# Where the halves of the split weights lie in SBUF, in which order the short products take them, and three load buffers for four

## The chip, the cores and the metric

The kernel runs on one core of a Trainium2 chip. The time is the device time of one execution in microseconds (us); lower is better. Before the change the median of two runs is 2517.6 us (2517.24 and 2517.97).

## The reference

The reference is a two-layer decoder trunk on 256 tokens of width 2048, all in float32. The first layer mixes tokens with a Mamba-2 block, the second with causal attention over one key/value block; each is followed by a residual layer norm and a gated feed-forward block with a depthwise convolution. Cut to the matrix products, which are nearly all of the work:

```python
zxbcdt = x @ w_in                          # 2048 -> 10304   (Mamba-2)
mix    = y @ w_out                         # 4096 -> 2048
u      = causal_dwconv(x @ w_up) ; ffn = (silu(gate) * val) @ w_down   # 2048 -> 11264, 5632 -> 2048, twice
kv     = h @ w_kv ; q = h @ w_q ; mix = out @ w_o
h      = layer_norm(alpha * h + f(h))      # after each of the four blocks
```

## The kernel before, in words

**Products in three passes.** TensorE multiplies in a rounded float32 type, so every operand is split in two: a high part (the value rounded) and a low part (what the rounding left). A product is then high times high, plus low weights times high activations, plus high weights times low activations.

**Steps.** All weights are packed by the host into 881 tiles of 128 partitions by 1024 columns (512 KB each) in the order of use; one tile is one *step*. For every step `load` (L172 to L180) issues one DMA on the SP queue into a `raw` buffer. `split` (L182 to L211) makes the two parts: ScalarE copies `raw` to the rounded type into a `hi` tile (L209), VectorE subtracts it from `raw` into a `lo` tile (L210), and then the next `load` is issued. There are `RAW` = 4 `raw` buffers and `LA`+1 = 4 `hi` and 4 `lo` tiles. A load has to wait until the subtraction that last read its buffer is done; loads stand on the SP queue in program order with the few other transfers of that queue (the input `x`, the constants `cols`, the norm's vectors and residuals).

**Two kinds of chunk.** A chunk is 512 output columns; its steps run one behind the other. In mode X (`half`, L221) activations are the stationary operand and weights stream. In mode W, 560 of the 881 steps (the Mamba-2 input but for one step, keys, queries, and all but the first feed-forward chunk of each layer), weights are the stationary operand: `some` (L250) issues for one step eight products of one part. With the high part (L266) a product streams 512 columns, the high and the low activations at once; these are the *long* products. With the low part (L269) it streams only the 256 columns of the high activations; these are the *short* products. Each product is a weight load of 128x128 and a matmul.

**Order of long and short.** `kinds` (L157) and `whole` (L283) arrange that the two parts alternate in opposite order from step to step, so that equal kinds meet: in the Mamba-2 chunks sixteen short products in a row, then sixteen long ones; in the other (`paired`) W chunks thirty-two and thirty-two. In the first chunk (`calm`) they alternate eight by eight. By the program's order there are 199 runs of short products: 92 of 32, 85 of 16 and 22 of 8 (the first chunk, and where other work of TensorE stands in between).

**Addresses.** Call the place of a tile's first byte within 256 bytes of its partition its *position*, in units of 64 bytes (0 to 3); 64 float32 columns are 256 bytes (`LINE`), and each product's 128 stationary columns are 512, so products of one contiguous tile all have one position. By the allocation, the activations `hT` (first byte 21632) and the `hi` tiles (75904, then every 4096) are at position 2. The `lo` tiles begin at 92480 (then every 4352), position 1; in mode W the low part is shifted by `LINE // 2`, 128 bytes, in every second step, and so lies at positions 1, 3, 1, 3 from step to step, in the first chunk always at 3. In mode X it is shifted to position 2.

**Norms.** Behind three of the four blocks the layer norm (`Norm`, L422, put in order by `chain`, L918) turns the result into the next block's `hT`; there the steps' high and low parts are written into free parts of `hT` (`spare`), and the queues carry the residuals besides the weights.

Of the kernel before, what the change touches and what calls it, by code (L numbers as in the profile page):

```python
# [18 lines left out]
F32 = mybir.dt.float32  # L19
F32R = mybir.dt.float32r  # L20
# [4 lines left out]
P = 128  # L25
D = 2048
S = 256
# [12 lines left out]
NC = 512  # L40
HC = NC // 2
NEG = -1.0e30
LINE = 64
# [6 lines left out]
    N_COL += _n // P  # L50

LA = 3
RAW = 4
WARM0 = 18
HEAD, TAIL = 3, 4
LAST = 8
# [3 lines left out]
def chunks():  # L60

    z, b, c, dt = 0, 2 * DI, 2 * DI + NG * DS, 2 * DI + 2 * NG * DS

    def some(mode, name, layer, c0, n, nk):
        return [(mode, name, layer, c0 + i * NC, nk, False) for i in range(n)]

    def ffn(layer):
        up = [some(m, "ffn_w_up", layer, c + j * NC, 1, KD)[0] for j in range(DFF // NC)
              for m, c in (("W" if j else "X", 0), ("W", DFF))]
        return up + some("X", "ffn_w_down", layer, 0, 4, KF)  # L70

    out = some("W", "mamba_w_in", 0, b, 2, KD)
    out[0] = out[0][:5] + (True,)
    out += some("H", "mamba_w_in", 0, dt, 1, KD) + some("W", "mamba_w_in", 0, c, 2, KD)
    for g in range(NG):
        out += some("W", "mamba_w_in", 0, DI + g * NC, 1, KD) + some("W", "mamba_w_in", 0, z + g * NC, 1, KD)
    out += some("X", "mamba_w_out", 0, 0, 4, DI // P) + ffn(0)
    out += some("X", "w_kv", None, D, 1, KD) + some("W", "w_kv", None, 0, 4, KD) + some("W", "attn_w_q", 0, 0, 4, KD)
    return out + some("X", "w_kv", None, D + NC, 3, KD) + some("X", "attn_w_o", 0, 0, 4, KD) + ffn(1)
# [12 lines left out]
def yoco_kernel(ctx: ExitStack, tc: tile.TileContext, x, lmg, lmb, lfg, lfb, x_t, columns, w, out):  # L92
    nc = tc.nc
    base = ctx.enter_context(tc.tile_pool(name="base", bufs=1))
    wts = ctx.enter_context(tc.tile_pool(name="wts", bufs=LA + 1))
# [30 lines left out]
    steps, plan = [], chunks()  # L126
# [39 lines left out]
    raw_t, hi_t, lo_t = {}, {}, {}  # L166
    spare = {}
    gap = []
    calm = []
    pos = {"split": 0, "load": 0}  # L170

    def load():  # L172
        i = pos["load"]
        if i >= n_steps:
            return
        pos["load"] += 1
        t = wts.tile([P, 2, NC], F32, tag="raw", name="raw", bufs=RAW)
        for e in (slice(0, 1), slice(1, 2)) if i == 0 else (slice(0, 2),):
            nc.sync.dma_start(t[:, e], w[i][:, e])
        raw_t[i] = t  # L180

    def split():  # L182
        i = pos["split"]
        pos["split"] += 1
        t = raw_t.pop(i)
        if i in spare:
            h, l = (bufs["h"][:, k:k + 2].rearrange("p k a t -> p k (a t)") for k in (spare[i], spare[i] + 2))
        else:
            h = wts.tile([P, 2, NC], F32R, tag="hi", name="hi")
            if not gap:  # L190
                gap.append(wts.tile([P, LINE * 3 // 4], F32R, tag="gap", name="gap", bufs=1))
            l = wts.tile([P, 2 * NC + LINE], F32R, tag="lo", name="lo")
            ch, s = steps[i]
            if len(gap) < 2:
                gap.append(wts.tile([P, LINE // 4], F32R, tag="gap2", name="gap2", bufs=1))

            o = LINE // 4 if ch.mode != "W" else LINE // 2 if s % 2 or ch in calm else 0
            l = l[:, o:o + 2 * NC].rearrange("p (a n) -> p a n", a=2)
        hi_t[i], lo_t[i] = h, l
        if steps[i][0].mode == "H":  # L200
            for a, w in enumerate((h, l)):
                v = t[:, a].rearrange("p (k n) -> p k n", k=8)
                w = w.rearrange("p a (k e n) -> p (a k) e n", e=2, n=NC // 8)
                nc.scalar.copy(w[:, :, 0], v)
                nc.vector.tensor_sub(w[:, :, 1], v, w[:, :, 0].bitcast(F32))
            return load()
        for e in ((0,), (1,)) if i < 2 else ((0, 1),):
            sl = slice(e[0], e[-1] + 1)
            nc.scalar.copy(h[:, sl], t[:, sl])  # L209
            nc.vector.tensor_sub(l[:, sl], t[:, sl], h[:, sl].bitcast(F32))  # L210
        load()  # L211

    def splits(i, most=2):

        for _ in range(1 if steps[i][0] in calm else most):
            j = pos["split"]
            ahead = LA + 1 + sum(i <= k < j for k in spare)
            if j < min(i + ahead, n_steps) and (j in spare or sum(k not in spare for k in hi_t) < LA + 1):
                split()
# [30 lines left out]
    def some(ch, s, p):  # L250

        i = ch.first + s
        nj = ch.nj
        w = ((hi_t, lo_t)[p][i]).rearrange("p a (k n) -> p a k n", n=nj * P)
        k0, half = ch.place(s)
        banks = [p[:, j, :] for p in ch.part[half:] for j in range(2)]
        first = ch.kinds(s)[0] == p
        for kk in range(ch.per):
            k = k0 + kk
            a, b = divmod(kk, ch.per // 2)  # L260
            begins, ends = first and k == 0, not first and k == ch.nk - 1
            for j in range(nj):
                yield
                js = slice(j * P, (j + 1) * P)
                if p == 0:
                    nc.tensor.matmul(banks[j], w[:, a, b, js], ch.x.both(k), start=begins, stop=ends,  # L266
                                     skip_group_check=True)
                else:
                    nc.tensor.matmul(banks[j][:, :S], w[:, a, b, js], ch.x.hi(k), start=begins, stop=ends,  # L269
                                     skip_group_check=True)  # L270

    def beside(i):

# [9 lines left out]
    def whole(i):  # L283

        ch, s = steps[i]
        if ch.mode == "H":
            return beside(i)
        a, b = ch.kinds(s)
        if not ch.paired:
            order = [(s, a), (s, b)]  # L290
        elif s % 2 == 0:
            order = [(s, a), (s + 1, a)]
        else:
            order = [(s - 1, b), (s, b)]
        late = ch.paired and s % 2
        n = len(order) * ch.per * ch.nj
        c = 0
        for t, p in order:
            for _ in some(ch, t, p):
                if c == (n // 2 if late else n * 3 // 8):  # L300
                    if late:
                        done(i - 1)
                    run(mid, i)
                    splits(i)
                c += 1
        if not ch.paired or late:
            done(i)
# [274 lines left out]
    calm.append(chB[0])  # L582
    put_x(0)
    split()
    put_x(2)
    split()
    for p in range(2, 8):
        amid(p - 2, put_x, 2 * p)
# [382 lines left out]
    def gb_ffn(c):  # L971
        return pool[f"ffn{int(0 if 'ffn0' in pool else 1)}"][1].tile([P, 2, NC], F32, tag="gb", name="gb", bufs=3)

    def gb_last(c):
        return gb_ffn(c) if c < 3 else wts.tile([P, 2, NC], F32, tag="raw", name="gb", bufs=RAW)

# [152 lines left out]
    for h in range(HEADS):  # L1129
        i, j = divmod(h, 4)  # L1130
# [87 lines left out]
```

## Time and profile before

| | |
|---|---|
| median of two runs | 2517.6 us |
| the profiled execution: its own time | 2516.88 us |
| its span, first to last instruction | 2514.6 us |
| matmuls of TensorE | 13983 |
| of these long products of W steps (L266) | 4480 |
| short products of W steps (L269) | 4480 |
| splits on ScalarE (L209) and VectorE (L210) | 869 of 881 steps in the largest group |
| weight loads by DMA | 880 of 512 KB, median 3.9 us from issue to landing |

PE is TensorE's matmuls, PEld its weight loads, ACT ScalarE, DVE VectorE, POOL GpSimd, SP the queue that issues the DMAs. In the rows of a group stand line, engine, operation, tiles, the shapes, the count, and then busy us and mean ns of one. The duration of a matmul in the trace holds its way through the array; the next one begins earlier, so the pace is the distance of the starts, not the duration. In the chain of waits a row is start, length, engine and line, and the number of instructions: there the starts follow one another, and length by count is the pace. In a timeline row the length runs from the first start to the last end, one duration more than the pace alone gives. The change is far below what the page's tenths show, so those two views in short windows carry the reading.

### The profile page before, as it was taken

How to read it: one execution, taken by the hardware profiler on the slowest of the kernel's cores; microseconds unless marked ns; L12 is line 12 of the kernel's file. 1: busy time of each engine (PE TensorE's matmuls, PEld its weight loads, DVE VectorE, ACT ScalarE, POOL GpSimd, SP SyncE). 2: the span in 40 equal slices, each digit the busy share in tenths (PEclk: the TensorE clock that was granted, in tenths of full speed). 3: DMA queues.
4: the chain of work that ended last, by engine and by line, in shares of the span. 5: the costliest groups of instructions: out<-in, count | busy, mean ns of one | idle time of the engine just before them, and what ended most of it. 6: DMA issues, size and time to landing. Idle time of an engine off the chain costs nothing.

```text
span 2514.6 us, 36085 instructions
## 1 busy us (share of the span) xinstructions
PE 2502.2 (100%) x13983; PEld 2175.0 (86%) x13983; DVE 1657.7 (66%) x2140; ACT 1365.5 (54%) x1790; POOL 76.4 (3%) x96
## 2 busy tenths in 40 slices
PE   9999999999999999999999999999999999999998
PEld 8888888888888888888888888888888888888887
DVE  7878888755666767675445646645767676765545
ACT  6677787643465555554333445543556555554333
POOL 0000000000200000000000200000200000000001
PEclk9999999999999999999999999999999999999999
DMA  7656655666666555556676655556656665566664
GB/s 259 207 188 203 211 190 189 202 209 222 212 207 193 193 192 191 195 185 201 209 227 205 212 194 172 160 178 227 220 192 197 194 192 194 186 198 204 198 228 161
DMA packets 141739, 502.59 MB, mean 200 GB/s; under 512 B 15856, under 2 KB 16368, under 8 KB 141568
## 3 DMA queue, kind: packets, MB, share of 16 engines
q1 hardware_dynamic: 136448, 482.92, 58.8%
q0 software_dynamic: 4832, 16.85, 2.2%
q8 instruction: 109, 1.79, 0.3%
q14 instruction: 62, 0.51, 0.1%
q10 hardware_dynamic: 288, 0.52, 0.1%
HBM read 491.77 MB, written 8.45 MB: 199 GB/s over the span
## 4 chain that ended last, share of the span: by engine, by line
PE 99%; DMA 0%; DVE 0%; SPq 0%; issue 0%; ACT 0%
PE acc L266 40%; PE acc L269 20%; PE acc L231 11%; PE acc L232 11%; PE acc L236 11%; PE acc L804 1%; PE tp L406 0%; PE tp L236 0%; PE tp L232 0%; PE tp L231 0%; DMA raw<-in_w 0%; PE tp L813 0%; PE acc L787 0%; PE tp L1083 0%; PE tp L1117 0%; PE tp L1109 0%
## 5 line engine op out<-in xcount | busy, mean ns | idle before, releaser
L210 DVE TENSOR_TENSOR lo<-raw,hi 128x1024 fp32r<-128x1024 f32 (+1 forms) x869 | 1059.6, 1225 | 726.5 <-ACT hi L209 598.5
L209 ACT CAST hi<-raw 128x1024 fp32r<-128x1024 f32 (+1 forms) x869 | 909.1, 1049 | 832.0 <-PE acc L236 366.8
L266 PE MATMUL acc<-hT,hi 128*128 128x512 f32 x4480 | 1058.3, 391 | 0.9 <-ACT hi L209 0.4
L266 PEld LDWEIGHTS acc<-hT,hi 128*128 128x128 f32 x4480 | 826.3, 188 | 165.6 <-ACT hi L209 1.8
L269 PEld LDWEIGHTS acc<-hT,lo 128*128 128x128 f32 x4480 | 543.4, 188 | 15.5 <-issue 1.2
L269 PE MATMUL acc<-hT,lo 128*128 128x256 f32 x4480 | 549.5, 278 | 0.0
L232 PE MATMUL acc<-lo,gT 128*128 128x512 f32 (+1 forms) x678 | 254.5, 378 | 0.0
L231 PE MATMUL acc<-hi,gT 128*128 128x512 f32 (+1 forms) x678 | 254.1, 377 | 0.0
L236 PE MATMUL acc<-hi,gT 128*128 128x512 f32 (+1 forms) x678 | 200.8, 377 | 0.0
L232 PEld LDWEIGHTS acc<-lo,gT 128*128 128x128 f32 x678 | 127.6, 188 | 23.2
L231 PEld LDWEIGHTS acc<-hi,gT 128*128 128x128 f32 x678 | 127.6, 188 | 23.1
L236 PEld LDWEIGHTS acc<-hi,gT 128*128 128x128 f32 x678 | 124.9, 188 | 23.9
L232 PE MATMUL acc<-lo,yT 128*128 128x512 f32 (+1 forms) x270 | 98.6, 369 | 0.0
L231 PE MATMUL acc<-hi,yT 128*128 128x512 f32 (+1 forms) x270 | 98.5, 369 | 0.0
L231 PE MATMUL acc<-hi,hT 128*128 128x512 f32 x192 | 78.8, 410 | 0.0
L236 PE MATMUL acc<-hi,yT 128*128 128x512 f32 (+1 forms) x270 | 77.7, 369 | 0.0
L232 PE MATMUL acc<-lo,hT 128*128 128x512 f32 x192 | 75.4, 393 | 0.0
L636 DVE SCALAR_TENSOR_TENSOR g<-u,cols,g 128x254 f32<-128x254 f32 (+1 forms) x176 | 73.3, 477 | 2.8 <-ACT g L631 2.7
L609 DVE TENSOR_TENSOR u<-u,acc 128x512 f32<-128x512 f32 x108 | 73.4, 681 | 2.3 <-ACT u L608 1.4
L1033 ACT CAST gT<-v 128x512 fp32r<-128x512 f32 x44 | 27.3, 621 | 84.5 <-DVE v L1032 84.5
L636 DVE SCALAR_TENSOR_TENSOR v<-u,cols,v 128x254 f32<-128x254 f32 (+1 forms) x176 | 73.1, 478 | 0.0
L468 POOL TENSOR_TENSOR rs<-rs,mhalf 128x1 f32<-128x1 f32 x8 | 7.4, 930 | 1984.9 <-DVE nb L469 1984.9
(223 smaller groups left out, 1910.7 us busy)
## 6 DMA issues: line engine op xcount, KB each, us to landing
raw<-in_w SPq DMA_DIRECT2D x880, 512.0 KB, 3.9
mA<-acum_d POOLq DMA_DIRECT2D x16, 512.0 KB, 6.4
hres<-r POOLq DMA_DIRECT2D x12, 512.0 KB, 6.8
r<-hres SPq DMA_DIRECT2D x12, 512.0 KB, 4.6
eA<-acum_d POOLq DMA_DIRECT2D x16, 128.0 KB, 7.3
r<-in_x SPq DMA_DIRECT2D x4, 512.0 KB, 5.5
gb<-in_ln_mix_g SPq DMA_DIRECT2D x8, 256.0 KB, 5.2
gb<-in_ln_mix_b SPq DMA_DIRECT2D x8, 256.0 KB, 5.4
```

The costliest lines, as they stand in the source:

```text
L209: nc.scalar.copy(h[:, sl], t[:, sl])
L210: nc.vector.tensor_sub(l[:, sl], t[:, sl], h[:, sl].bitcast(F32))
L231: nc.tensor.matmul(a, th, h[:, kk, sl], start=k == 0, stop=False)
L232: nc.tensor.matmul(a, th, l[:, kk, sl], start=False, stop=False)
L236: nc.tensor.matmul(a, ch.x.lo(k)[:, ts], h[:, kk, sl], start=False, stop=k == ch.nk - 1)
L266: nc.tensor.matmul(banks[j], w[:, a, b, js], ch.x.both(k), start=begins, stop=ends, skip_group_check=True)
L269: nc.tensor.matmul(banks[j][:, :S], w[:, a, b, js], ch.x.hi(k), start=begins, stop=ends, skip_group_check=True)
L468: nc.gpsimd.tensor_tensor(self.rs[:, h, :], self.rs[:, h, :], mhalf[:, 0, :], op=OP.pow)
L609: nc.vector.tensor_add(dst, dst, p[:, :, :S])
L636: nc.vector.scalar_tensor_tensor(d, u[:, i % 2, :S - k], c1(self.at_w, w[n - 1 - k] + self.ia + i), d, op0=OP.mult, op1=OP.add)
L804: nc.tensor.matmul(ps[64 * q:64 * q + 64, c, j * P:(j + 1) * P], G[g]["xdt"][:, c, h * 64:(h + 1) * 64], G[g]["A", c][:, h, :], start=True ...
L1033: nc.scalar.copy(h, v[:, sl])
```

## The change

Three things change in the code.

1. `RAW` goes from 4 to 3: one `raw` buffer of 4096 bytes a partition less. The four `hi` tiles grow by 1024 bytes each, so `lo` and everything behind it stays where it was; the `hi` tiles lie 5120 bytes apart and still begin at position 2.
2. In mode W the `lo` tile is two halves of 544 columns, of which 512 are used: the first half of every step lies at position 1 and the second at position 3. `some` takes the eight short products in the order 0, 1, 4, 5, 2, 3, 6, 7, so their positions are 1, 1, 3, 3, 1, 1, 3, 3 in every step, the first chunk's too.
3. In the W steps whose high part is used right behind short products (every second step of the Mamba-2 chunks, every fourth of the paired ones: 180 steps) the high part is laid out in four pieces of 256 columns. The first piece begins `o`, the second `e`, the third and fourth `d` further, each with a position of its own out of four: 64 combinations, drawn by a hash of the step's number. Two products fall to each piece; their order is as before. ScalarE's copy and VectorE's subtraction take the tile in four pieces of 256 there; numbers of instructions, sizes and waits stay.

```diff
-RAW = 4
+RAW = 3
...
-            h = wts.tile([P, 2, NC], F32R, tag="hi", name="hi")
+            h = wts.tile([P, 2 * NC + 4 * LINE], F32R, tag="hi", name="hi")
+            ch, s = steps[i]
+            if ch.mode == "W" and s % (4 if ch.paired else 2) == (2 if ch.paired else 1):
+                o, d, e = (LINE // 4 * ((i * 2654435761 >> 9) // 4 ** m % 4) for m in range(3))
+                e += HC
+                d += NC
+                while d < 2 * e:
+                    d += LINE
+                while o + 2 * d > 2 * NC + 4 * LINE:
+                    d -= LINE // 4
+                h = h[:, o:o + 2 * d].rearrange("p (a n) -> p a n", a=2)[:, :, :2 * e]
+                h = h.rearrange("p a (b n) -> p a b n", b=2)[:, :, :, :HC]
+            else:
+                h = h[:, :2 * NC].rearrange("p (a n) -> p a n", a=2)
...
-            o = LINE // 4 if ch.mode != "W" else LINE // 2 if s % 2 or ch in calm else 0
-            l = l[:, o:o + 2 * NC].rearrange("p (a n) -> p a n", a=2)
+            if steps[i][0].mode == "W":
+                l = l.rearrange("p (a n) -> p a n", a=2)[:, :, :NC]
+            else:
+                l = l[:, LINE // 4:LINE // 4 + 2 * NC].rearrange("p (a n) -> p a n", a=2)
...
+            u, v, r = t[:, sl], h[:, sl], l[:, sl]
+            if len(h.shape) == 4:
+                u, r = (y.rearrange("p a (b n) -> p a b n", b=2) for y in (u, r))
+            nc.scalar.copy(v, u)
+            nc.vector.tensor_sub(r, u, v.bitcast(F32))
...
+        order = [(a, b, j) for a in range(2) for b in range(ch.per // 2) for j in range(nj)]
+        if p == 1:
+            order = [order[i] for i in (0, 1, 4, 5, 2, 3, 6, 7)]
+        for a, b, j in order:
+            yield
+            k = k0 + a * (ch.per // 2) + b
```

More of the change, by code (lines that the diff above doesn't have):

```diff
@@ L192, in split @@
             l = wts.tile([P, 2 * NC + LINE], F32R, tag="lo", name="lo")
-            ch, s = steps[i]
             if len(gap) < 2:
                 gap.append(wts.tile([P, LINE // 4], F32R, tag="gap2", name="gap2", bufs=1))
-            o = LINE // 4 if ch.mode != "W" else LINE // 2 if s % 2 or ch in calm else 0
-            l = l[:, o:o + 2 * NC].rearrange("p (a n) -> p a n", a=2)
+            if steps[i][0].mode == "W":
+                l = l.rearrange("p (a n) -> p a n", a=2)[:, :, :NC]
+            else:
+                l = l[:, LINE // 4:LINE // 4 + 2 * NC].rearrange("p (a n) -> p a n", a=2)
         hi_t[i], lo_t[i] = h, l
@@ L208, in split @@
             sl = slice(e[0], e[-1] + 1)
-            nc.scalar.copy(h[:, sl], t[:, sl])
-            nc.vector.tensor_sub(l[:, sl], t[:, sl], h[:, sl].bitcast(F32))
+            u, v, r = t[:, sl], h[:, sl], l[:, sl]
[3 more added lines that the diff above has]
+            nc.vector.tensor_sub(r, u, v.bitcast(F32))
         load()
@@ L253, in some @@
         nj = ch.nj
-        w = ((hi_t, lo_t)[p][i]).rearrange("p a (k n) -> p a k n", n=nj * P)
+        w = (hi_t, lo_t)[p][i]
+        if len(w.shape) == 3:
+            w = w.rearrange("p a (b n) -> p a b n", b=2)
         k0, half = ch.place(s)
@@ L257, in some @@
         first = ch.kinds(s)[0] == p
-        for kk in range(ch.per):
-            k = k0 + kk
-            a, b = divmod(kk, ch.per // 2)
-            begins, ends = first and k == 0, not first and k == ch.nk - 1
[L262 to L270, printed above, removed]
+        order = [(a, b, j) for a in range(2) for b in range(ch.per // 2) for j in range(nj)]
[4 more added lines that the diff above has]
+            k = k0 + a * (ch.per // 2) + b
+            begins, ends = first and k == 0, not first and k == ch.nk - 1
+            c, j0 = divmod(b * nj * P + j * P, HC)
+            js = slice(j0, j0 + P)
+            if p == 0:
+                nc.tensor.matmul(banks[j], w[:, a, c, js], ch.x.both(k), start=begins, stop=ends,
+                                 skip_group_check=True)
+            else:
+                nc.tensor.matmul(banks[j][:, :S], w[:, a, c, js], ch.x.hi(k), start=begins, stop=ends,
+                                 skip_group_check=True)
     def beside(i):
```

## The prediction

> **What bounds the kernel now.** I read the page first, for the bound and the clock, then the waits of TensorE.
>
> ```profile
> span 2514.6 us, 36085 instructions
> PE 2502.2 (100%) x13983; PEld 2175.0 (86%) x13983; DVE 1657.7 (66%) x2140; ACT 1365.5 (54%) x1790; POOL 76.4 (3%) x96
> PEclk9999999999999999999999999999999999999999
> PE 99%; DMA 0%; DVE 0%; SPq 0%; issue 0%; ACT 0%
> L266 PE MATMUL acc<-hT,hi 128*128 128x512 f32 x4480 | 1058.3, 391 | 0.9 <-ACT hi L209 0.4
> L269 PE MATMUL acc<-hT,lo 128*128 128x256 f32 x4480 | 549.5, 278 | 0.0
> ...
> PE tp L581 <- POOL ident masks.py:199: 1.4, 1, 1.4
> PE acc L266 <- ACT hi L209: 0.4, 1, 0.4
> PE acc L266 <- DVE hT L569: 0.3, 1, 0.3
> ```
>
> TensorE is the chain from end to end, at full clock. The last three rows are all that it waited for in the whole execution: 2.1 us, all at the start. So no transfer and no other engine can give time back; the change can win only in the pace of the products themselves, and it can lose wherever it makes TensorE wait. A busy 100% does not say that this pace is the best one. For that I read the chain of waits in a paired W stage and in a Mamba-2 stage, and the timeline inside two runs.
>
> ```profile
> 806.71 3.66 PE acc L269 x32
> 810.38 7.28 PE acc L266 x32
> ...
> 337.19 1.85 PE acc L269 x16
> 339.04 3.65 PE acc L266 x16
> ...
> 20.15 0.94 PE acc L269 x8
> ```
>
> ```profile
> 806.55 0.99 PE L269 MATMUL acc<-hT,lo 128*128 128x256 f32 x7
> 808.06 1.18 PE L269 MATMUL acc<-hT,lo 128*128 128x256 f32 x9
> 810.21 1.32 PE L266 MATMUL acc<-hT,hi 128*128 128x512 f32 x5
> 812.28 1.75 PE L266 MATMUL acc<-hT,hi 128*128 128x512 f32 x7
> ```
>
> A timeline row holds one duration besides its paces (278 and 391 ns by the two groups). The run's first seven short products come every (990 - 278) / 6 = 119 ns; nine from the later part every (1180 - 278) / 8 = 113 ns. The long run's first five come every (1320 - 391) / 4 = 232 ns, seven later ones every (1750 - 391) / 6 = 226.5 ns. So there are two paces for one shape, a slow one where a run begins and a fast one. As floors I take 226.6 ns and half of it, 113.3. Then the 32 short products lose 3.66 - 32 x 0.1133 = 0.034 us, the 16 lose 1.85 - 16 x 0.1133 = 0.037, so a run loses about 36 ns whatever its length, and eight of one position lose 0.94 - 0.906 = 0.034. The 32 long ones lose 7.28 - 7.25 = 0.03 us, the 16 lose 3.65 - 3.626 = 0.024: 28 ns a run. That is what the change can reach: 199 x 36 ns = 7.2 us in the short runs and 180 x 28 ns = 5.0 us in the long runs whose first step is cut in pieces, 0.5% of the time together.
>
> **The change part by part. Short products.** Nothing is added or removed: 4480 products with the same operands; weight loads read other addresses in another order. Today a run's first eight lie at one position and the slow pace lasts through these eight, to be gone at the ninth, where the position moves by 128 bytes; it does not come back at the 17th or 25th, where it moves again. After the change it moves at the third. If the move ends the slow pace, two products at 119 and one or two on the way down are left, some 10 of the 36 ns, and 199 x 26 ns = 5.2 us are saved. The other bound is that the slow pace ends by itself after eight; or, worse, that moving every two products keeps it up. For this the trace has a row of a kind: in the last steps of a mode X block products of 256 columns whose operands are all at position 2 run at a slow pace that never ends:
>
> ```profile
> 663.24 0.28 PE L231 MATMUL acc<-hi,yT 128*128 128x256 f32 x1
> 663.36 0.28 PE L232 MATMUL acc<-lo,yT 128*128 128x256 f32 x1
> 663.48 0.28 PE L231 MATMUL acc<-hi,yT 128*128 128x256 f32 x1
> 663.60 0.28 PE L232 MATMUL acc<-lo,yT 128*128 128x256 f32 x1
> ```
>
> They stand 0.12 us apart, one behind the other. All 4480 at 119 ns would be 4480 x 5.7 = 25.5 us of loss against 7.2 today, 18 us more. Bounds: -7.2 to +18 us. I take -5.2, by the nearest rows, the two inside the same run: the fast pace begins at a move of 128 bytes and outlasts two more of them.
>
> A rule of the Trainium skill speaks against all of this: "TensorE: Matmul & The Clock Gate", section "Step-by-step: what each phase is for", says that loading weights and streaming the moving operand read through two independent ports, so that the next weights' load takes nothing from the running matmul. By it no position would matter and this term would be 0. The 119 and 113 ns for one shape at one clock do not go with it, unless the slow pace is only a beginning that ends by itself.
>
> **Long products in pieces.** Again the same products; the 180 steps have up to four positions instead of one. Today's 28 ns arise at constant position 2, and they end by themselves after five products. Every place where a row shows the slow pace set in is a change between long and short, which is also a move of 64 bytes (position 2 to 1 or 3, 3 to 2); moves of 128 bytes did no harm. Of the 64 combinations half move by 64 or 192 bytes between the first two pieces, and about half end at an odd distance from position 2, where the next, uncut, step begins. Bounds: all of the 28 saved, 180 x -28 ns = -5.0 us; or all eight at 232 instead of 226.5 and another 28 ns at the next step, 8 x 5.7 + 28 - 28 = +46 ns, +8.2 us. I take +10 ns a step, +1.8 us: nearer to today's loss than to either end, and on its bad side, since the draw mixes good and bad moves and today's constant position heals after five.
>
> The cut copies cost nothing on the path: the numbers of instructions and columns are the same, ScalarE is busy 54% and VectorE 66%, and TensorE waited 0.4 us for a split in the whole run. Without that cover, a copy that took a tenth longer would be 0.1 us on 180 steps, 18 us.
>
> **One load buffer less.** A load now waits for the subtraction three steps before it, not four. Queued behind it on SP are the next loads, at the start also the last part of `x` and `cols`, and behind the blocks the norm's residuals and vectors; behind a late load wait ScalarE's copy and all that stands after it on ScalarE, then VectorE's subtraction, then TensorE.
>
> ```profile
> L179 SPq DMA_DIRECT2D raw<-in_w x882: 327/328/677, 1.3 to 2484.6; - x177
> DMA to landing us min/median/max: 3.0/3.9/9.3
> L210 DVE TENSOR_TENSOR lo<-raw,hi 128x1024 fp32r<-128x1024 f32 (+1 forms) x869 | 1059.6, 1225 | 726.5 <-ACT hi L209 598.5
> L209 ACT CAST hi<-raw 128x1024 fp32r<-128x1024 f32 (+1 forms) x869 | 909.1, 1049 | 832.0 <-PE acc L236 366.8
> ACT hi L209 <- DMA raw<-in_w: 42.0, 28, 4.3
> ```
>
> In the steady state one buffer's round is 3.9 + 1.05 + 1.23 = 6.2 us, so three buffers bring a step every 2.1 us; TensorE needs one every 2514.6 / 881 = 2.85 us. The four `hi` buffers put a split up to three steps, some 8 us, ahead of its use, so a load that lands a step later is late for ScalarE but not for TensorE. Two places have less. At the start the fourth load leaves at 4.92 today:
>
> ```profile
> 4.92 0.68 SPq L179 DMA_DIRECT2D raw<-in_w  x1
> 5.64 0.66 SPq L564 DMA_DIRECT2D x<-in_x_t  x1
> 7.51 11.75 SPq L179 DMA_DIRECT2D raw<-in_w  x5
> 3.62 7.74 DMA raw<-in_w
> ```
>
> It will leave where the fifth leaves now, at 7.51, 2.6 us later, and the last of `x` behind it. But the load of 3.62 lands only 7.74 us later, at 11.36: the transfers stand in line, and one that joins at 7.51 is still in that line. So I expect 0 to 1 us here. The other places are the three norms:
>
> ```profile
> 687.20 1.05 ACT L209 CAST hi<-raw 128x1024 fp32r<-128x1024 f32 x1 [2.01 <-DMA raw<-in_w]
> 692.12 2.11 ACT L209 CAST hi<-raw 128x1024 fp32r<-128x1024 f32 x2 [3.88 <-DMA raw<-in_w]
> ```
>
> ScalarE waits 2.0 and 3.9 us for late weights there already, and TensorE does not feel it. Bounds: nothing at both places (not below nothing: a load never leaves earlier than before), or a full shift reaching TensorE. That is two loads at the start, 2 x 2.6 us, and at each norm 3 us, less than the longest wait there: 5.2 + 9 = 14 us. I take +1 us, near the lower end, because of the steady surplus of 2.85 over 2.1.
>
> **Sum** against the profiled execution, 2516.9 us (span 2514.6 and 2.3 around it): 2516.9 - 5.2 + 1.8 + 1.0 = 2514.5. The median before is 0.7 us above that execution, so I forecast 2515.2, 2515 us.
>
> **The rivals.** (a) *The slow pace ends by itself*, after about 36 ns of loss, wherever the positions are. For it: the long runs heal at constant position, and runs of 16, of 32 and of eight lose the same 0.034 to 0.037. Against it: the eight at one position keep an average of 0.94 / 8 = 117.5 ns, so they are slow to their end, and the X rows never heal. Then the short term is 0: 2517.6 + 1.8 + 1.0 = 2520.4, slower than before. The page's rule of independent ports would come to this time too. (b) *The load ring reaches TensorE*, at the first steps and behind the three norms, with the full 14 us: 2517.6 - 5.2 + 1.8 + 14 = 2528. It decides as soon as a load that leaves later takes as long as it does now, instead of waiting less in line. The waits of 2.0 and 3.9 us behind the norm speak for it; that TensorE does not wait there at all today speaks against. (c) *The pieces keep the slow pace up* in all eight products and hand it on: 2517.6 - 5.2 + 8.2 + 1 = 2521.6. (d) *The pieces heal the long runs too*, as moves of 128 bytes do in the short ones: 2517.6 - 5.2 - 5.0 + 1 = 2508.4. That the change doesn't do what it says is excluded for the order and the addresses, which the built program fixes.
>
> **How the numbers follow.** The forecast has 0.50, and its own range is 2512 to 2518; (a) 0.17, (b) 0.10, (c) 0.10, (d) 0.13. The range reaches from (d), 2508, past (c) to 2525, which leaves out most of (b) and the case where moving every two products keeps the short ones slow, up to 2536, which I put inside (a)'s chance as its tail. A difference of 2% is 50 us, about what a measurement of this kernel can tell from no change. No term sums to that: both upper bounds of the pace and the ring together are 18 + 8 + 14 = 40 us. So within 2% has 0.97; slower 0.02, for a ring that delays TensorE in every stage; faster 0.01.
>
> **What would show it.** Right: runs of 32 short products at 3.63 to 3.64 in the chain of waits and of 16 at 1.82; wrong, if they stay at 3.66 and 1.85, or grow. The long runs behind them: 7.28 should become 7.27 to 7.31, unequal from run to run because of the draw; a constant value would say that position is nothing to them. The list of TensorE's waits should stay as short as it is; rows "PE acc L266 <- ACT hi" with more than 1 us, at 5 to 30 us or behind the norms, would show the ring. The waits of ScalarE for raw should grow from 42.0 us without harm. If TensorE's products are slower in mode X, where nothing moved, the prediction is wrong at its root.

## The result, and the profile after

The changed kernel takes 2537.84 us (two runs, 2536.64 and 2539.04) against 2517.6 us: a ratio of 1.0082, with a 95% interval of 1.0065 to 1.0098. It is 20 us slower, above the range of the prediction. The profiled execution took 2539.04 us, its span is 2536.9 us, 22.3 us more than before.

The page of the changed kernel: busy time, clock, the chain by engine, and the two groups of W products (L287 is the long one, L290 the short one).

```profile
span 2536.9 us, 36083 instructions
PE 2509.5 (99%) x13983; PEld 2174.2 (86%) x13983; DVE 1657.9 (65%) x2140; ACT 1367.6 (54%) x1790; POOL 76.1 (3%) x96
PE 87%; DMA 4%; DVE 4%; ACT 3%; issue 2%; POOL 0%; SPq 0%; ACTq 0%; DVEq 0%; POOLq 0%
L287 PE MATMUL acc<-hT,hi 128*128 128x512 f32 x4480 | 1064.4, 392 | 0.9 <-DVE hT L590 0.9
L290 PE MATMUL acc<-hT,lo 128*128 128x256 f32 x4480 | 544.6, 277 | 0.0
```

The two groups show that both kinds of product moved, in opposite ways: busy time 549.5 to 544.6 us for the short ones, 1058.3 to 1064.4 for the long ones. That nearly cancels. The new thing is the chain: TensorE holds 87% of it and not 99%; transfers, VectorE and ScalarE have come in. The waits say where: first TensorE's five longest rows (sum, count, longest, in us), then the row of ScalarE that grew most.

```profile
PE tp L427 <- POOL r L517: 4.7, 3, 1.6
PE tp L869 <- DVE sq L863: 3.6, 5, 0.9
PE tp L427 <- DVE r L501: 2.6, 2, 2.3
PE tp L427 <- issue: 1.9, 1, 1.9
PE acc L249 <- DVE hT L227: 1.5, 2, 0.8
```

```profile
ACT hi L226 <- DMA raw<-in_w: 194.6, 154, 5.2
```

Only the last of TensorE's five rows is a wait for a weight's half. L427 are the norms' transposes, L869 is the mean-square product of a Mamba-2 group, and both wait for other work of VectorE and GpSimd. The prediction had looked for the ring in rows `PE acc <- ACT hi` of more than 1 us, and there is none. ScalarE's wait for weights went from 42.0 us in 28 waits to 194.6 us in 154.

Taken product by product (both kernels issue the same 13983 matmuls in the same order; distance from one start to the next, after less before; more than 40 ns counted as a wait), the 22.3 us of the span come out so:

```
pace of the short products   -4.7 us
pace of the long products    +4.9 us
waits: start (to 13 us)      +1.0
       Mamba-2 groups        +5.6
       three norms           +2.3 +5.4 +4.9
       last chunk            +3.1
```

Of the second and the third norm's waits about 1.5 us each are not standing still: there products run at half clock behind a pause (last section).

### The profile page after: what moved, and what is told of

Read it like the earlier page. It is cut to its first block, busy times and chain, and to the rows that moved or that the text cites. A ratio compares the mean times of both kernels' runs of the same rounds, so it can differ in the third digit from the quotient of the medians.

```text
span 2536.9 us, 36083 instructions
## 1 busy us (share of the span) xinstructions
PE 2509.5 (99%) x13983; PEld 2174.2 (86%) x13983; DVE 1657.9 (65%) x2140; ACT 1367.6 (54%) x1790; POOL 76.1 (3%) x96
## 4 chain that ended last, share of the span: by engine, by line
PE 87%; DMA 4%; DVE 4%; ACT 3%; issue 2%; POOL 0%; SPq 0%; ACTq 0%; DVEq 0%; POOLq 0%
PE acc L287 35%; PE acc L290 18%; PE acc L249 10%; PE acc L248 10%; PE acc L253 10%; DMA raw<-in_w 4%; DVE lo L227 1%; ACT hi L226 1%; ACT mA L773 0%; DVE xc L657 0%; PE tp L253 0%; PE tp L249 0%; PE tp L248 0%; DMA gb<-in_ln_mix_g 0%; DVE mA L792 0%
## 5 line engine op out<-in xcount | busy, mean ns | idle before, releaser
L287 PE MATMUL acc<-hT,hi 128*128 128x512 f32 x4480 | 1064.4, 392 | 0.9 <-DVE hT L590 0.9
L287 PEld LDWEIGHTS acc<-hT,hi 128*128 128x128 f32 x4480 | 827.5, 188 | 170.0 <-ACT hi L226 1.3
L290 PEld LDWEIGHTS acc<-hT,lo 128*128 128x128 f32 x4480 | 538.8, 188 | 15.8 <-issue 0.9
L290 PE MATMUL acc<-hT,lo 128*128 128x256 f32 x4480 | 544.6, 277 | 0.0
```

Source lines behind the costliest of these rows:

```text
L287: nc.tensor.matmul(banks[j], w[:, a, c, js], ch.x.both(k), start=begins, stop=ends, skip_group_check=True)
L290: nc.tensor.matmul(banks[j][:, :S], w[:, a, c, js], ch.x.hi(k), start=begins, stop=ends, skip_group_check=True)
```

## The experiments

**One load buffer less, alone.** From the kernel before:

```diff
-RAW = 4
+RAW = 3
```

> Only one load buffer less. If the ring alone makes TensorE wait, the 22.3 us of stalls of the changed kernel come back without its other parts: 2537 to 2542 us, with TensorE waiting in front of the mean-square products of the Mamba-2 groups, in the three norms and in the last chunk. If the cut copies of the high parts delay the splits and so are needed for the stalls: 2525 or less.

Measured: 2538.11 us (four runs, 2535.83 to 2539.12), ratio 1.0081 (1.0066 to 1.0096). TensorE's longest waits:

```profile
PE tp L406 <- POOL r L496: 5.2, 3, 2.5
PE tp L848 <- DVE sq L842: 5.0, 7, 0.9
PE tp L406 <- issue: 2.3, 1, 2.3
```

The missing buffer alone makes the whole loss, at the same places: 8.9 us in the Mamba-2 groups, 9.3 in the norms, 1.9 in the last chunk by the same count. The pieces are not needed for it.

**Three buffers and the pieces, short products as before.** From the changed kernel:

```diff
-                l = l.rearrange("p (a n) -> p a n", a=2)[:, :, :NC]
+                o = LINE // 2 if s % 2 or ch in calm else 0
+                l = l[:, o:o + 2 * NC].rearrange("p (a n) -> p a n", a=2)
...
-        if p == 1:
-            order = [order[i] for i in (0, 1, 4, 5, 2, 3, 6, 7)]
```

> Three load buffers and the high parts in pieces; the short products as before. If the three parts add, the long products lose 4.9 us more than before as in the changed kernel, beside the stalls of three buffers alone (20 us, 2538.1): 2543 us, 5 us above both that run and the changed kernel. If the pieces also make the stalls longer, by slower copies: above 2547.

Measured: 2539.08 us (2538.05 to 2542.07), ratio 1.0087 (1.0072 to 1.0102). The median is 1 us above that of three buffers alone, not 5; but the runs of each spread over 3 to 4 us, so the time alone does not tell. The products do: the long ones lose 5.0 us more than before, as in the changed kernel, and the waits sum to 20.1 us as with three buffers alone (20.6). So the pieces cost pace, and no longer waits show. That execution is the longest of its four, though. If the pieces cost the 5.0 us in all of them, the waits of the median are nearer to 16 us: they differ by some us from execution to execution.

**Three buffers, the mean-square products a step later.** From the kernel with three buffers alone, all of `z_rms` to `z_split` moved by a step except in the last group:

```diff
-        at(s0 + 23, z_rms, g)
+        at(s0 + 23 + (g < NG - 1), z_rms, g)
...
```

> Three load buffers and nothing else of the change, but the mean-square products of the Mamba-2 groups (and what hangs on them) are put one step later, except in the last group. If TensorE there waits for ScalarE's and VectorE's other work that stands behind late weights, and not for the weights, one step more hides it: the stalls of 0.4 to 1.2 us in front of these products go, some 6 of the 20 us, 2532 us; the norms' and the start's stay. If the weights themselves are late, the wait moves to the next product that needs them: 2538.

Measured: 2536.75 us (four runs, 2533.73 to 2542.38), ratio 1.0083 (1.0067 to 1.01). The runs spread over 9 us, so the time does not decide between the two cases. The waits do:

```profile
PE acc L269 <- DVE lo L210: 4.0, 6, 1.2
PE tp L406 <- POOL r L496: 3.8, 3, 1.5
```

The waits in front of the mean-square products are gone, and six waits for low parts of splits stand in their place. My theory that one step of room hides the delay falls, and the other case came, in which the wait moves on. In front of the longest of the six (1.16 us, at 348.17) the weight's subtraction starts on VectorE behind that of `z_split` (L875, 1.22 us), which the edit had moved there, and two more operations. I read this as the queues of ScalarE and VectorE being behind as a whole, so that TensorE meets whatever of them it needs first.

**Three buffers, the Mamba-2 decay tiles set and not loaded.** This asks why they are behind in that stage: it leaves 32 transfers of the POOL queue out.

```diff
-            nc.gpsimd.dma_start(t, bass.AP(tensor=s.tensor, offset=s.offset, ap=[[0, P], [S, 8], [1, P]]))
+            nc.gpsimd.memset(t, 0.0)
...
-        for q in range(2):
-            nc.gpsimd.dma_start(e[64 * q:64 * q + 64], bass.AP(tensor=s.tensor, offset=s.offset + q * S,
-                                                               ap=[[0, 64], [2 * S, 4], [1, P]]))
+        nc.gpsimd.memset(e, 0.0)
```

> Three load buffers and nothing else of the change; the decay tiles of the Mamba-2 groups (mA and eA, 32 DMAs on the POOL queue) are set to zero by GpSimd and not loaded, so the output is another one. If the stalls of the Mamba-2 stage come from weight loads that take 7 to 9 us beside these transfers, and that three buffers no longer cover, the 8.9 us of that stage go and the norms' and the last chunk's 11 us stay: 2529 us. If three buffers are too few there at the usual 3 to 4 us too, because ScalarE and VectorE are busy: 2538 as with three buffers alone.

Measured: 2532.2 us (2531.6 to 2533.75), ratio 1.0057 (1.004 to 1.0074). By the count of products the Mamba-2 stage waits 0.0 us now, and the norms and the last chunk keep theirs (15.1 us in this execution, more than the 11 expected, so the whole time fell by 6 and not by 9; about 4 of the 15.1 are products at half clock, with three buffers alone 1.5). In the window from 105 to 500 us, the time from issue to landing of the weight loads, with three buffers alone and then without the decay transfers:

```profile
DMA to landing us min/median/max: 3.0/4.0/9.7
```

```profile
DMA to landing us min/median/max: 3.0/3.3/4.9
```

and ScalarE's waits for them in that window (sum, count, longest), in the same order:

```profile
ACT hi L209 <- DMA raw<-in_w: 43.9, 32, 4.8
```

```profile
ACT hi L209 <- DMA raw<-in_w: 27.2, 25, 2.0
```

The longest load and the longest wait both fall to about half. The edit also removes ScalarE's waits for the decay tiles themselves, with three buffers alone 3.6 us in five. They are not the cause in that trace: in front of each of its seven longest Mamba-2 waits of TensorE stands a wait of ScalarE for a weight (1.4 to 2.4 us), and within 7 us none for a decay tile.

The kernel before has loads of 9.3 us in this window too, and waits only twice: its fourth buffer sent the load a step earlier.

**The short products alone**, with four buffers. From the kernel before, the changed kernel's `lo` layout and order, and nothing else.

```diff
-            o = LINE // 4 if ch.mode != "W" else LINE // 2 if s % 2 or ch in calm else 0
-            l = l[:, o:o + 2 * NC].rearrange("p (a n) -> p a n", a=2)
+            if ch.mode == "W":
+                l = l.rearrange("p (a n) -> p a n", a=2)[:, :, :NC]
+            else:
+                l = l[:, LINE // 4:LINE // 4 + 2 * NC].rearrange("p (a n) -> p a n", a=2)
...
+        if p == 1:
+            order = [order[i] for i in (0, 1, 4, 5, 2, 3, 6, 7)]
```

> Only the short products' positions and their order are changed; four load buffers, high parts as before. If a move of 128 bytes ends the slow pace, the 199 short runs save the 5 us that the changed kernel's short products show against those of before, and nothing else moves: 2512.5 us, short runs of 32 at 3.64 in the chain of waits. If the slow pace ends by itself and the saving came from something else in the changed kernel: 2517.6. TensorE waits for nothing new in either case.

Measured: 2512.83 us (ten runs, 2511.86 to 2513.05), ratio 0.9981 (0.9971 to 0.999). In the chain of waits:

```profile
804.18 3.64 PE acc L272 x32
807.82 7.28 PE acc L269 x32
```

The short run is 3.64 and not 3.66, the long one stays at 7.28. All short products together are 4.9 us faster than before. This part of the change is a gain.

**The low parts at one position**, with four buffers:

```diff
-            o = LINE // 4 if ch.mode != "W" else LINE // 2 if s % 2 or ch in calm else 0
+            o = LINE // 4 if ch.mode != "W" else 0
```

> Four load buffers, the low parts of all mode W steps at position 1, no move within a run; the rest as before. If only a move of the position ends the slow pace, it lasts through the runs of 16 and 32: 92 x 24 + 85 x 8 = 2888 products more at 118 instead of 113.3 ns, +13.6 us, 2531 us, runs of 32 at 3.77 in the chain of waits. If it ends by itself after some 36 ns: 2517.6 and 3.66 as before.

Measured: 2535.75 us (one run), and in the chain:

```profile
813.33 3.77 PE acc L269 x32
817.10 7.30 PE acc L266 x32
```

3.77 is what 32 products at 118 ns make: without a move the slow pace lasts through the whole run. The rival that it ends by itself falls. The short products cost 12.7 us, close to the 13.6 expected. What was not expected is the 7.30: the long products lose another 4.1 us in all. Either the slow pace in which a run of short products ends is handed on to the next run, or the position of its last product does it, which is now 1 and was 3; this run does not part the two. The other 2 us are waits at the start and, 1.3 us, at the third norm, so with four buffers TensorE can wait there too.

**The high part in two halves**, at positions 1 and 2, with four buffers and the short products as in the change. In the changed kernel's trace every run of 32 long products carries the loss of one draw. Three of them from its chain of waits, whose cut steps have their four pieces at positions 0, 2, 2, 0, then 2, 1, 0, 3 and 1, 1, 2, 2:

```profile
862.85 7.34 PE acc L287 x32
...
961.35 7.34 PE acc L287 x32
...
1114.71 7.26 PE acc L287 x32
```

By the distances of starts, over the draws of a combination in runs that no other work of TensorE interrupts (loss over 226.57 ns a product, in the cut step's eight products and in the rest of the run):

```
1 1 2 2   +7  and  +1 ns      2 2 2 2   +27 and  +1
0 0 2 2  +16  and  +1         1 0 3 2   +36 and +26   (drawn most often, ten times)
3 1 2 0  +41  and +47         2 0 0 2   +62 and +33   (one of the two worst)
```

In such runs of one length the loss repeats within 2 ns for the draws of these combinations. So one was taken for all 180 steps. The first half starts at position 1, the second 528 columns later; the uncut steps' tiles at position 2. For the room of 1 KB one constant of 512 bytes (`tri`) was moved into a pool that closes after the Mamba-2 block.

```diff
-            h = wts.tile([P, 2, NC], F32R, tag="hi", name="hi")
             if not gap:
                 gap.append(wts.tile([P, LINE * 3 // 4], F32R, tag="gap", name="gap", bufs=1))
+            h = wts.tile([P, 2 * NC + LINE], F32R, tag="hi", name="hi")
...
+            if ch.mode == "W" and s % (4 if ch.paired else 2) == (2 if ch.paired else 1):
+                h = h[:, :2 * NC + LINE // 2].rearrange("p (a n) -> p a n", a=2)[:, :, :NC]
+            else:
+                h = h[:, LINE // 4:LINE // 4 + 2 * NC].rearrange("p (a n) -> p a n", a=2)
...
-    tri = base.tile([P, P], F32, name="tri")
+    tri = mp.tile([P, P], F32, name="tri")
```

> Four load buffers, short products as in the change, and in the 180 steps behind short products the high part in two halves at positions 1 and 2, the combination that lost 8 ns instead of 29 in the changed kernel's trace (its room comes from a constant tile moved to a pool that is closed later). If the loss belongs to the combination: 2517.6 - 5 - 180 x 0.021 = 2508.8 us, long runs behind short ones at 7.26 in the chain. If the loss of a combination in the changed kernel came from what lay around it: 2512.5, long runs at 7.28.

Measured: 2509.34 us (six runs, 2509.12 to 2509.8), ratio 0.9967 (0.9956 to 0.9979). The long run is 7.26 in its chain:

```profile
807.52 7.26 PE acc L273 x32
```

The long products are 3.3 us faster than before and the short ones 4.9. This version beats both kernels, the one before by 8 us.

## Why the prediction was wrong

**The bound** was read right: nothing but TensorE's pace could be won, and the loss is time in which TensorE waits, but for some 3 us at half clock behind two of the pauses.

**The short products**: forecast -5.2 us, measured -4.7 in the changed kernel and -4.9 alone. The reason given, that the move of 128 bytes ends the slow pace, is shown by the constant position: there the addresses of the stationary operand, and nothing else, cost the short products 12.7 us. In the trace of the short products alone the slow pace is gone at the third product of a run, where the position now moves. The Trainium skill ("TensorE: Matmul & The Clock Gate", section "Step-by-step: what each phase is for") says that loading the next weights takes no SBUF read bandwidth from the running matmul. The prediction read this as saying that no position would matter, and read so it does not agree with the 12.7 us; what in the machine makes the difference no run here shows.

**The pieces**: forecast +1.8 us, measured +4.9. The sign was right, and the value was mis-sized: 27 ns a step in place of 10. I had reasoned from odd and even moves, and the table above does not follow that rule, so the sign did not come from a mechanism that I had understood: 1 1 2 2, the best, has an odd move in it, and 2 0 0 2 with even moves only is one of the two worst.

**One load buffer less**: forecast +1 us, bounded at +14; measured 22.3 us of waits in the changed kernel and 20.6 alone. This is the step that failed, and in three ways.

First, it set 3.9 us, the median over the whole run, into one buffer's round and called the result a surplus everywhere. In the Mamba-2 groups loads take up to 9.7 us, as the window shows; by the same sum such a load makes a step every (9.7 + 1.05 + 1.23) / 3 = 4.0 us, against 2.85 needed. That stage was not on the list of tight places at all.

Second, it said that a late load "is late for ScalarE but not for TensorE". The splits indeed are seldom late for TensorE. But ScalarE and VectorE work in order, as the rows below show, and the sentence before had named what is queued there without asking who waits for that. One of the groups in the changed kernel, ScalarE, VectorE and TensorE:

```profile
417.12 1.05 ACT L226 CAST hi<-raw 128x1024 fp32r<-128x1024 f32 x1 [1.96 <-DMA raw<-in_w]
418.08 0.40 ACT L862 CAST sq<-sz 128x256 fp32r<-128x256 f32 x1
418.20 1.23 DVE L227 TENSOR_TENSOR lo<-raw,hi 128x1024 fp32r<-128x1024 f32 x1 [0.95 <-ACT hi L226]
...
419.35 0.42 DVE L863 TENSOR_TENSOR sq<-sz,sq 128x256 fp32r<-128x256 f32 x1
...
419.82 0.39 PE L869 MATMUL tp<-sq,mean 128*128 128x256 f32 x1 [0.91 <-DVE sq L863]
```

ScalarE waits 1.96 us for a weight tile. Behind it stands the small copy of 0.40 us that the mean square needs; the low part of that waits on VectorE behind the weight's subtraction; and TensorE stands still for 0.91 us. The same at a norm, in the chain of waits (start, length, what):

```profile
1393.02 5.07 DMA raw<-in_w
...
1398.18 1.06 ACT hi L226
...
1399.26 0.06 DVE lo L227
...
1400.40 0.69 DVE r L471
...
1402.55 1.07 POOL rs L489
```

The load lands at 1398.08, the copy and the subtraction follow, and the norm's add (L471) starts only at 1400.40, behind the subtraction; from there the norm runs through to the transpose that TensorE waits for. That it is this transfer and not VectorE's load that is missing at the norms is the chain's account; no experiment took the norms apart.

Third, even the upper bound was too low. It had one shift of 3 us for each norm, 9 us, where 12.6 were lost, 3 of them at half clock, and nothing for the last chunk, where 3.1 us were lost behind a load that took 6.69 us.

**The rivals.** (b), the ring, is what happened, at the norms that it named and at two places more, with 20 to 22 us for its 14. Its condition held: the loads did not become shorter by leaving later (longest 9.3 us before and 9.5 in the changed kernel). (a) and (d) fall by the experiments; (c) was the right direction at 60% of its price. At the start, where I had worked out why nothing is lost, 1.0 us was, and part of that is a first transfer of `x` that landed 0.7 us later. In the three runs with four buffers the same stretch lies between 0.3 us below and 1.1 us above the kernel before, so this loss is not shown to be the ring's.

## What to carry to other kernels

A prefetch ring is sized by the longest transfer of each stage and not by the median of the run, and a late tile costs what stands behind it on the in-order engines, which is to be listed operation by operation with who waits for it. A trade of buffer space for layout should be priced on both sides: here 4 KB a partition bought 180 layouts and lost 20 us, while the useful one needed 1 KB that could be found elsewhere. When a layout has many free parameters, a draw that mixes them in one kernel is a good measurement and a poor kernel: read the table from the trace, then fix the best.

## What the runs showed of the hardware that was not expected

**Addresses set the pace of matmuls.** With the same shapes, order and clock, 128-column weight loads at four positions within 256 bytes make between 8 and 96 ns of loss in a run of long products (over 226.57 ns each), the same within some ns each time for the same positions. What the cut step leaves is carried on within the run: after 1 1 2 2 and after 1 0 3 2 the rest lies at position 2 alike, and loses 1 and 26 ns.

**Half a clock after a short pause.** Behind the longest wait of the changed kernel TensorE's products run at half pace. The windows give length, then busy time of TensorE, its weight loads, VectorE, ScalarE and GpSimd, then granted clock, DMA share and GB/s.

```profile
1401.90:1404.50 2.60, 0.30 (x4) 0.10 (x2) 2.10 (x6) 0.59 (x1) 1.24 (x2) 1.00 0.44 176
1404.60:1406.00 1.40, 1.40 (x13) 1.40 (x13) 0.79 (x3) 0.71 (x2) 1.20 (x1) 0.93 0.00 0
1406.00:1409.40 3.40, 3.40 (x12) 2.80 (x12) 2.57 (x7) 0.00 (x0) 2.13 (x3) 0.53 0.00 0
```

TensorE stands idle for 2.3 us, and soon after it starts again its 512-column products come every 0.43 us in place of 0.23. The trace's record of the granted clock has 0.5 from 1405.79 to 1409.21 us and 1.0 around it; the 0.93 and 0.53 are means of windows that cut across the change. The same comes at the third norm, behind a pause of 1.94 us (0.5 from 1791.50 to 1794.91). Each time the products lose about 1.5 us there, so a wait costs more than its length.

The records also show which pauses do this. From the first full clock to the last, the changes of the granted clock in a run lie whole multiples of 3.413 us apart (in the changed kernel 1396.05, 3.41, 382.29, 3.41 and 737.28 us, which are 409, 1, 112, 1 and 216 of them). On that grid, in the five traces with three buffers, each of the seven windows with 1.94 to 2.33 us of idle TensorE was followed by half clock, and none at full clock with 1.76 us or less was (idle by the trace, where the ends of matmuls are modelled). With three buffers alone a pause of 2.48 us at the second norm passed without it: a border of the grid parted it into 1.43 and 1.06 us. The Trainium skill, "TensorE: Matmul & The Clock Gate", section "What's actually happening", states that the clock falls to one half after at least one idle window of about 3.4 us; here a window that was idle for 1.94 us of its 3.41 was enough.
